# Hybrid attention layer: x's first tile on ScalarE's queue, the first weights rounded on VectorE, loads of x and weights in turn, and an order planned with the trace's figures

## The chip, the cores and the metric

The kernel runs on one core of one Trainium2 chip. The metric is device microseconds of one execution. The kernel before took 437.04 us, the median of three runs (436.71 to 437.82).

## The reference

One decoder layer on x of 512 tokens by 1024 channels, in float32. x is RMS-normalised and multiplied by one large input projection `w_in`; the result is cut into the inputs of two attention mixers and their gates.

```python
h = rms_norm(x, norm_w[l])
proj = h @ w_in[l]
o_a = moba_mixer(rms_norm(heads(q_a), ...), rms_norm(heads(k_a), ...), heads(v_a), bias_a)
k_cmp = rms_norm(compress(heads(kc), ...), k_norm_cmp[l]); v_cmp = compress(heads(vc), ...)
o_b = nsa_mixer(rms_norm(heads(q_b), ...), k_cmp, v_cmp, ..., heads(vwn), gate_b, bias_b)
y_a = o_a * jax.nn.silu(z_a); y_b = o_b * jax.nn.silu(z_b)
g_m = jax.nn.sigmoid(gate_m)
merged = g_m[..., :D] * (y_a @ w_branch_a[l]) + g_m[..., D:] * (y_b @ w_branch_b[l])
x = x + merged @ w_out[l]
```

Mixer A has 8 heads of 64 channels over all earlier tokens, with a relative-position bias; mixer B has 8 heads in two groups and three branches (compressed, selected and window), each with its own keys and values, summed with sigmoid gates. At 512 tokens the choice of blocks takes in every earlier block, so both mixers are causal attention with a bias, and B has a short compressed branch besides.

## The kernel before

**Precision.** Products that must be exact to float32 are made of three: every operand is split into a rounded part ("hi", written by a cast) and a remainder ("lo", written by a subtraction), and TensorE adds hi·hi, lo·hi and hi·lo into one PSUM tile (`mm3`, L420 to L434). So each weight tile of 128 x 512 costs one cast (L396, on ScalarE), one subtraction on VectorE (L406) and its matmuls. x is split in the same way, eight tiles of 128 channels by 512 tokens (`x_split`, L506 to L513), into `hh` and `hl`, with `norm_w` multiplied in. The division by the rms is applied later, to the results.

**Stages.** A few small matmuls on a tile of zeros stand first (L502, `NWARM` of them). Then comes the first projection, `qk0` (`gemm_first`, L683), which walks over the eight k tiles as they arrive: per tile four matmuls hi·hi, four with x's lo, four with the weights' lo. The others follow in the list `ORDER` (L632): token projections (`qk1`, `v`, `qb`, `kb`, `vb`) through `gemm_tok`, channel ones (`kc`, `vc`, the gates `za0` to `zb3`) through `gemm_chan`. Two entries of the list are not projections: `bias` makes the rows of the relative-position table (`bias_rows`, L863, one matmul, then a store to DRAM from which each head's table T is loaded), and `rows` spreads 1/rms over all partitions (`x_rows`, L577, two matmuls). Then come, per 128 output channels, a merge gate and a branch product (`gmgate`, `branch`, the loop at L1422 for A and at L1425 for B), and the output projection in seven products (L1568 on).

Attention runs between these. A unit is one head of A or one head and branch of B (24 in all). Per block of 128 queries: scores in PSUM (L1094, or L1092 for two branches at once), bias added and the minimum taken on VectorE (L1114), exp on ScalarE (L1125), hi and lo of the probabilities (L1132 and L1136), a DMA transpose, and the product with v (L1149). After a unit's last block `o_out` scales the output, and `y_try` multiplies in the gate and splits it for the branch product (L1187 to L1194). The first branch product of B waits for all of B's outputs.

**What sets the order.** The instruction order on every engine is fixed when the program is built, by a small simulation in the kernel itself. Each chain of operations (`Chain`) carries a cost in nanoseconds per engine ("A" ScalarE, "D" or "d" VectorE, "P" or "p" GpSimd), and a heap issues what is ready first. DMAs have a model of their own (`dma`, L231): issue time on SP, 1000 ns, then the transfer one after the other, 1700 ns to arrive. TensorE's order is the loop at L1637: several generators (`Run`) such as projections F, scores A, values V wait for conditions; of those whose condition holds since at least their margin (`MARGIN` 300 ns, `LATE_A` for scores, `LATE_V` for values, `LATE_S` for the scales of v), the one with the least virtual time goes next. If none has waited that long, the one that became ready first goes. Engines then run their lists in order and wait on semaphores for data, so a wrong cost changes no result but can put an instruction where its data is not there yet.

**Loads.** All DMAs are issued by SP. Weight tiles come through `Stream` (L331): `bufs` limits how far loads run ahead. At the start the loads stand in the order x0, w0, x1, x2, w1, x3, x4, w2, x5, x6, w3, x7, w4 (L499 and L1619 to L1625). x0 brings `norm_w` in 8 more columns.

Of the kernel before, what the change touches and what calls it, by code (L numbers as in the profile page):

```python
# [47 lines left out]
NRAW = 6  # L48
NWARM = 38
LAT = 60  # L50
# [8 lines left out]
MARGIN = 300  # L59
LATE_A = 1000  # L60
LATE_V = 1500
LATE_S = 1000
# [41 lines left out]
def hybrid_kernel(ctx: ExitStack, tc: tile.TileContext, x, x0, xT, wtok, wchan, gains, w1,  # L104
# [125 lines left out]

    def dma(dst, src, n, t=None):  # L231

        nc.sync.dma_start(out=dst, in_=src)
        t = issue(now[0] if t is None else t, 420)
        free["Q"] = max(free["Q"], t + 1000) + max(450, n * P / 360)
        return free["Q"] + 1700
# [94 lines left out]
    class Stream:  # L331


        def __init__(w, tiles, bufs, hi, lo):
            w.tiles, w.bufs, w.mk_hi, w.mk_lo = tiles, bufs, hi, lo
            w.raw, w.out, w.chain, w.i, w.loaded, w.ahead, w.next = {}, {}, {}, 0, 0, 0, 0

# [41 lines left out]
        def split(w, upto):  # L379
            for i in range(w.next, min(upto, len(w.tiles))):  # L380
# [13 lines left out]
                def f(e, hi=hi, raw=raw):  # L394
                    if e is nc.scalar:
                        e.copy(hi, raw)  # L396
                    else:
                        e.tensor_scalar(hi, raw, 1.0, 1.0, op0=ALU.mult, op1=ALU.mult)
                c.do({"A": ca(n)}, f).mark((w, 0, i))
                if squares:  # L400
# [50 lines left out]
    nrx = cp.tile([P, NT], F32, name="nrx")  # L451
    R = cp.tile([P, S], F32, name="R")
    nc.scalar.activation(R[:, :8], mhalf, AF.Exp)
    kcs = cp.tile([P, 2, 2, C32], F16, name="kcs")
# [20 lines left out]
    def rsqrt_mean(c, dst, ss, n, w, parts=P):  # L475
        v = (lambda z: z() if callable(z) else z)
        c.do({"D": 70}, lambda e: e.tensor_scalar(v(ss), v(ss), 1.0 / n / QS ** 2, EPS / QS ** 2, op0=ALU.mult, op1=ALU.add))  # L477
        c.do({"p": 430 + 150 * w}, lambda e: e.tensor_tensor(v(dst), v(ss), mhalf[:parts, :w], op=ALU.pow))  # L478

# [10 lines left out]

    first = alloc("dst", "x0", (P, 2048))
    xts = [first[:, :S]] + [att("x", F32) for _ in range(1, KT)]
    xat = {}

    def load_x(k):
        xat[k] = dma(xts[k], xT[(k - 1) * P:k * P, :], 2048)

    now[0] = 700.0
    xat[0] = dma(first[:, :S + KT], x0, 2080)  # L499
    Chain(xat[0]).do({"p": 140}, lambda e: e.tensor_copy(w8, first[:, S:S + KT]))  # L500
# [130 lines left out]

    ORDER = "qk0 bias v rows kc vc qk1 za0 kb qb za1 vb za2 za3 zb0 zb1 zb2 zb3".split()  # L632
    ORDER_T = [n for n in ORDER if n not in ("bias", "rows")]
    tiles = []
    for n_ in ORDER_T:
        tiles += tok_tiles(n_) if n_ in tlay else chan_tiles(n_)
# [198 lines left out]
    def proj_v(name, tags="gggg"):  # L835
        toks[name], per, i = [None] * NT, 1 + (name == "vb"), int(name == "vb")
        n = S // per

        def emit(t, ps):
            if t % per == 0:  # L840
                two = att(name, F32).bitcast(F16)
                toks[name][t:t + per] = [two[:, 2 * n * k:2 * n * (k + 1)] for k in range(per)]
            z = toks[name][t].rearrange("p (h s d) -> p h s d", s=2, d=DH)
            src, r = ps[:, :n].rearrange("p (h d) -> p h d", d=DH), rv[:, i, t:t + 1]
            ch = Chain(now[0] + 230, held=("vs", name) not in done)
            if ch.held:
                vwait[name].append(ch)
            else:
                ch.t = max(ch.t, done["vs", name])
            ch.do({"A": 145 + 0.834 * n}, lambda e: e.activation(z[:, :, 0, :], src, AF.Copy, scale=r))  # L850
            ch.do({"D": 65 + 1.045 * n}, lambda e: e.scalar_tensor_tensor(  # L851
                z[:, :, 1, :], src, r, z[:, :, 0, :], op0=ALU.mult, op1=ALU.subtract), ps).mark(f"{name}.{t}")
        yield from gemm_tok(name, emit, tags)
# [28 lines left out]
    def load_bias(h):  # L882
# [4 lines left out]
        t = dma(T, bass.AP(tensor=row.tensor, offset=row.offset + P - 1,  # L887
                           ap=[[16 * TW - P // NG, NG], [-1, P // NG], [1, S]]), 2048)
        return T, t
# [146 lines left out]
    class Unit:  # L1036
# [70 lines left out]
        def bias(u, c, b, sps, frees, T, last=False):  # L1107
            z, L, st = {}, P * (b + 1), u.stats()

            def f(e):  # L1110
# [5 lines left out]
                if last:  # L1116
                    release(T, c.t)
            c.do({"D": cd(L)}, f, frees, "sb")
            return z
# [44 lines left out]
    def o_out(O, m, h):  # L1164
# [14 lines left out]
        def f(e):  # L1179
            e.scalar_tensor_tensor(y[row:row + 64, :], O[0:64, :], r[0:64], z["t"], op0=ALU.mult, op1=ALU.add)  # L1180
            release(O, ch.t)
        ch.do({"D": 602}, f, lambda: z["t"])
        if row:
# [222 lines left out]
    def gemms():  # L1406
        for n in ORDER:
            if n == "rows":
                yield from x_rows()
            elif n == "bias":  # L1410
                yield from bias_rows()
            elif n == "v":
                yield from proj_v("v", "ttto")
# [4 lines left out]
            elif n[0] == "z":  # L1418
                yield from zgate(n[1], int(n[2]))
            else:  # L1420
                yield from proj_norm(n, n == ORDER_T[0], "ttto" if n == ORDER_T[1] else "gggg")
        for j in range(8):  # L1422
# [195 lines left out]

    W.bufs += 1  # L1619
    for k in range(1, KT):  # L1620
        if k % 2:
            W.load()
        load_x(k)
    W.load()
    W.bufs -= 1  # L1625
    for k in range(KT):
# [6 lines left out]
    Z = Run(starts(), 100.0)  # L1633
    U = Run(itertools.chain(v_scale("v", "s"), v_scale("vb", "t")), 100.0, LATE_S)
    Y = Run(itertools.chain(*sides), SHARE_B)
    runs = [Z, X, U, B, V, A, Y, F, C]
    while any(r.live for r in runs):  # L1637
# [90 lines left out]
```

## Time and profile before

| what | value |
|---|---|
| median of the runs | 437.04 us |
| lowest, highest | 436.71, 437.82 us |
| the profiled execution | 437.77 us |
| its span, first to last instruction | 435.6 us |
| TensorE (PE) busy | 421.2 us, 97% |
| VectorE (DVE) busy | 367.5 us, 84% |
| ScalarE (ACT) busy | 309.6 us, 71% |
| GpSimd (POOL) busy | 33.4 us, 8% |
| DMA | 75.30 MB, 173 GB/s on average |
| granted TensorE clock | 0.999 |

The span is shorter than the execution's time by 2.17 us, which lie before the first and after the last instruction. Times in rows count from the span's start. In a timeline row stand start and length in microseconds, engine, source line, operation, the tile written and those read, shapes and the number of instructions merged; in brackets how long the engine was idle before and what ended that. PEld is TensorE's load of weights, which overlaps its matmuls; SPq and the like are the sequencers, where DMAs are issued. "Rounding" or "cast" in the text is the writing of a hi part.

### The profile page before, as it was taken

The numbers are of one execution on the slowest core, as the hardware profiler recorded it, in microseconds if no ns is written. First come the engines' busy times: TensorE is split into PE (matmuls) and PEld (weight loads), VectorE is DVE, ScalarE is ACT, GpSimd is POOL, SyncE is SP. The second block draws the span as 40 slices with busy tenths as digits, with TensorE's granted clock in tenths as the row PEclk, the third lists the DMA queues.
The fourth block names the chain that finished last, engine by engine and source line by source line (L and its number), as shares of the span: only waits on it lengthen the run. The fifth ranks groups of instructions, "written<-read, shape, count | busy, mean of one in ns | idle before, by whom it ended". The sixth has DMA issues, their size and how long they took to land.

```text
span 435.6 us, 7107 instructions
## 1 busy us (share of the span) xinstructions
PE 421.2 (97%) x2134; PEld 326.0 (75%) x2134; DVE 367.5 (84%) x952; ACT 309.6 (71%) x802; POOL 33.4 (8%) x37
## 2 busy tenths in 40 slices
PE   9999999999988999999999999989999999999996
PEld 7878776777956687877776666757778888888886
DVE  5969689999898989699999798879955877599993
ACT  7996668897896998378899888979842534354720
POOL 0026000113213221000000000000000000000000
PEclk9999999999999999999999999999999999999999
DMA  8852978679989989417769867786668399251143
GB/s 290 269 203 65 216 200 165 110 178 232 236 239 185 161 179 256 121 23 159 164 149 156 182 165 133 192 136 153 155 175 285 122 353 322 77 172 47 50 136 104
DMA packets 116693, 75.30 MB, mean 173 GB/s; under 512 B 89072, under 2 KB 92016, under 8 KB 116656
## 3 DMA queue, kind: packets, MB, share of 16 engines
q1 hardware_dynamic: 116656, 74.86, 68.2%
q8 instruction: 17, 0.28, 0.2%
q14 instruction: 20, 0.16, 0.1%
HBM read 51.11 MB, written 2.75 MB: 124 GB/s over the span
## 4 chain that ended last, share of the span: by engine, by line
PE 60%; DVE 21%; DMA 6%; ACT 6%; issue 4%; POOL 1%; SPq 1%; DVEq 0%; POOLq 0%
PE pgc L431 21%; PE pgt L431 12%; PE po L431 9%; PE pbr L431 8%; DMA dst<-sb 5%; PE pgf L694 5%; DVE sb L1114 4%; DVE wl L406 4%; DVE sb L1136 3%; PE O L1149 3%; PE sps L1094 3%; ACT wh L396 1%; ACT junk L404 1%; DVE vl L406 1%; DMA x<-in_xT 1%
## 5 line engine op out<-in xcount | busy, mean ns | idle before, releaser
L431 PE MATMUL pgc<-hh,wh 128*128 128x512 f32 x208 | 87.3, 419 | 0.0
L431 PE MATMUL pgc<-hl,wh 128*128 128x512 f32 x208 | 82.1, 395 | 0.0
L431 PE MATMUL pgc<-hh,wl 128*128 128x512 f32 x208 | 82.1, 395 | 0.0
L406 DVE TENSOR_TENSOR wl<-wr,wh 128x512 fp32r<-128x512 f32 (+1 forms) x112 | 72.7, 666 | 10.0 <-ACT wh L396 9.7
L396 ACT CAST wh<-wr 128x512 fp32r<-128x512 f32 (+1 forms) x112 | 64.9, 597 | 6.9 <-DMA wr<-in_wbr 4.4
L1125 ACT ACTIVATE sb<-sb,sst 128x512 f32<-128x512 f32 (+3 forms) x96 | 53.4, 556 | 20.5 <-DVE sst L1114 20.0
L1114 DVE CUSTOM_DVE_ANT_0 sb<-sps,T,gst 128x512 f32<-128x512 f32 (+3 forms) x96 | 51.6, 540 | 9.3 <-DMA dst<-sb 8.4
L431 PE MATMUL pgt<-wh,hh 128*128 128x512 f32 (+2 forms) x160 | 58.3, 365 | 0.5 <-DVE vb L851 0.3
L431 PE MATMUL pgt<-wl,hh 128*128 128x512 f32 (+2 forms) x160 | 56.3, 352 | 0.9 <-DVE wl L406 0.9
L431 PE MATMUL pgt<-wh,hl 128*128 128x512 f32 (+2 forms) x160 | 55.8, 349 | 0.0
L1132 ACT ACTIVATE sb<-sb,sst 128x512 f16<-128x512 f32 (+3 forms) x96 | 51.1, 553 | 6.3 <-DVE sst L1128 5.8
L1136 DVE SCALAR_TENSOR_TENSOR sb<-sb,sst 128x512 f16<-128x512 f32 (+3 forms) x96 | 51.4, 544 | 3.7 <-ACT sb L1132 3.3
L431 PEld LDWEIGHTS pgc<-hl,wh 128*128 128x128 f32 x208 | 39.0, 188 | 9.5
L431 PEld LDWEIGHTS pgc<-hh,wh 128*128 128x128 f32 x208 | 39.1, 188 | 8.9
L431 PEld LDWEIGHTS pgc<-hh,wl 128*128 128x128 f32 x208 | 39.1, 188 | 7.5
L1094 PE MATMUL sps<-qkt,qkt 128*128 128x384 f16 (+3 forms) x160 | 36.4, 318 | 3.4 <-DVE sst L1114 3.4
L478 POOL TENSOR_TENSOR nr<-nss,mhalf 128x8 f32<-128x8 f32 (+1 forms) x16 | 26.7, 1675 | 105.7 <-DVE nss L477 94.6
L431 PEld LDWEIGHTS pgt<-wl,hh 128*128 128x128 f32 x160 | 30.0, 188 | 5.9 <-DVE wl L406 2.0
L431 PEld LDWEIGHTS pgt<-wh,hh 128*128 128x128 f32 x160 | 30.1, 188 | 4.9 <-PE pgt L431 0.4
L431 PEld LDWEIGHTS pgt<-wh,hl 128*128 128x128 f32 x160 | 30.1, 188 | 3.4
L1094 PEld LDWEIGHTS <-qkt 128*128 128x128 f16 x160 | 11.3, 98 | 21.2 <-issue 12.2
L431 PE MATMUL pbr<-yh,wh 128*128 128x512 f32 x64 | 26.2, 409 | 0.0
(226 smaller groups left out, 789.1 us busy)
## 6 DMA issues: line engine op xcount, KB each, us to landing
wr<-in_wchan SPq DMA_DIRECT2D x52, 256.0 KB, 3.5
wr<-in_wtok SPq DMA_DIRECT2D x36, 256.0 KB, 4.1
wq<-in_wout SPq DMA_DIRECT2D x36, 256.0 KB, 3.7
T<-rtab SPq DMA_DIRECT2D x16, 256.0 KB, 4.1
wr<-in_w SPq DMA_DIRECT2D x16, 256.0 KB, 3.5
wr<-in_wbr SPq DMA_DIRECT2D x16, 256.0 KB, 3.9
xr<-in_x SPq DMA_DIRECT2D x8, 256.0 KB, 5.7
x<-in_xT SPq DMA_DIRECT2D x7, 256.0 KB, 4.8
```

The lines of the kernel that those rows point to most:

```text
L396: e.copy(hi, raw)
L404: d.do({"A": 190 + 0.834 * m}, lambda e, z=hi[:, o:o + m], y=junk[:, :m], g=g, acc=acc: e.activation(y, z.bitcast(F32), AF.Square, scale=g ...
L406: c.do(either(n), lambda e, hi=hi, lo=lo, raw=raw: e.tensor_sub(lo, raw, hi.bitcast(F32))).mark((w, 1, i))
L431: nc.tensor.matmul(dst, sts[i][a], mvs[i][b], start=(start and i == a == b == 0), stop=(stop and i == n - 1 and b == 1), skip_group_check= ...
L478: c.do({"p": 430 + 150 * w}, lambda e: e.tensor_tensor(v(dst), v(ss), mhalf[:parts, :w], op=ALU.pow))
L694: nc.tensor.matmul(ps[t][:, :n], (hl if a else hh)[:, k, t * P:(t + 1) * P], ws[k][b], start=(k == a == b == 0), stop=(k == KT - 1 and b = ...
L1094: nc.tensor.matmul(sps[:, :n].rearrange("p (t n) -> p t n", n=P), qs, k4[:, x, j, :b + 1], start=not x, stop=bool(x))
L1114: e.tensor_tensor_reduce(z["sb"], sps[:, :L], T[:, S - L:], scale=nrunscale, scalar=3e38, op0=ALU.add, op1=ALU.min, accum_out=st[:, 0, b:b ...
L1125: c.do({"A": 279 + 0.834 * L}, lambda e: e.activation(z["sb"], z["sb"], AF.Exp, bias=st[:, 0, b:b + 1], scale=-1.0, accum_out=st[:, 1, b:b ...
L1132: e.activation(z["pp"][:, :L], z["sb"], AF.Copy, scale=s_)
L1136: c.do({"d": 59 + cd(L)}, lambda e: e.scalar_tensor_tensor(z["pp"][:, L:], z["sb"], s_, z["pp"][:, :L], op0=ALU.mult, op1=ALU.subtract))
L1149: nc.tensor.matmul(out, v, u.moving(kb, i), start=(u.first and kb == i == 0), stop=(u.last and kb == 3 and i == 1 and not u.before))
```

## The change

- x's first tile is loaded by ScalarE's DMA queue, ahead of ScalarE's first activation; its issue costs SP nothing in the plan.
- The cast of the first weight tile (and of no other) goes to VectorE, at a planned 205 + 0.54 n ns.
- Loads of weights and x stand in turn: w0, x1, w1, x2, and so on, with up to six weight tiles ahead instead of five.
- `bias_rows` and `x_rows` leave the list `ORDER` and become runs of their own: the first ahead of the scales of v in run U, the second in a new run O_.
- In `ORDER`, `vb` moves behind `za2`.
- Planned costs: GpSimd's power 430 to 700 ns plus 150 per column, VectorE's score step and two more steps 57 ns longer, a table load twice as long in the queue.
- `LATE_A` goes from 1000 to 1300, `LATE_V` from 1500 to 2000, `NWARM` from 38 to 33.

```diff
-NWARM = 38
+NWARM = 33
-LATE_A = 1000
-LATE_V = 1500
+LATE_A = 1300
+LATE_V = 2000
-    def dma(dst, src, n, t=None):
-        nc.sync.dma_start(out=dst, in_=src)
-        t = issue(now[0] if t is None else t, 420)
+    def dma(dst, src, n, t=None, engine=None):
+        (engine or nc.sync).dma_start(out=dst, in_=src)
+        t = issue(now[0] if t is None else t, 0 if engine else 420)
...
+            w.first = hi is None or w.bufs > 2
...
-                c.do({"A": ca(n)}, f).mark((w, 0, i))
+                c.do({"D": 205 + 0.54 * n} if w.first and not i else {"A": ca(n)}, f).mark((w, 0, i))
...
+    now[0] = 700.0
+    first = alloc("dst", "x0", (P, 2048))
+    xat = {0: dma(first[:, :S + KT], x0, 2080, None, nc.scalar)}
     nc.scalar.activation(R[:, :8], mhalf, AF.Exp)
...
-        c.do({"p": 430 + 150 * w}, ...)          # rsqrt_mean
+        c.do({"p": 700 + 150 * w}, ...)
...
-    first = alloc("dst", "x0", (P, 2048))
-    xat = {}
-    now[0] = 700.0
-    xat[0] = dma(first[:, :S + KT], x0, 2080)
...
-    ORDER = "qk0 bias v rows kc vc qk1 za0 kb qb za1 vb za2 za3 zb0 zb1 zb2 zb3".split()
+    ORDER = "qk0 v kc vc qk1 za0 kb qb za1 za2 vb za3 zb0 zb1 zb2 zb3".split()
...
-            ch.do({"D": 65 + 1.045 * n}, ...)    # proj_v, lo part
+            ch.do({"D": 122 + 1.045 * n}, ...)
-                           ap=[[16 * TW - P // NG, NG], [-1, P // NG], [1, S]]), 2048)
+                           ap=[[16 * TW - P // NG, NG], [-1, P // NG], [1, S]]), 4096)
-            c.do({"D": cd(L)}, f, frees, "sb")   # score step, L1114
+            c.do({"D": 57 + cd(L)}, f, frees, "sb")
-        ch.do({"D": 602}, f, lambda: z["t"])     # o_out
+        ch.do({"D": 659}, f, lambda: z["t"])
...
-    W.bufs += 1
+    W.bufs += 2
     for k in range(1, KT):
-        if k % 2:
-            W.load()
+        W.load()
         load_x(k)
-    W.load()
-    W.bufs -= 1
+    W.bufs -= 2
...
-    U = Run(itertools.chain(v_scale("v", "s"), v_scale("vb", "t")), 100.0, LATE_S)
+    U = Run(itertools.chain(bias_rows(), v_scale("v", "s"), v_scale("vb", "t")), 100.0, LATE_S)
+    O_ = Run(x_rows(), 100.0)
-    runs = [Z, X, U, B, V, A, Y, F, C]
+    runs = [Z, X, U, O_, B, V, A, Y, F, C]
```

More of the change, by code (lines that the diff above doesn't have):

```diff
@@ L477, in rsqrt_mean @@
         c.do({"D": 70}, lambda e: e.tensor_scalar(v(ss), v(ss), 1.0 / n / QS ** 2, EPS / QS ** 2, op0=ALU.mult, op1=ALU.add))
-        c.do({"p": 430 + 150 * w}, lambda e: e.tensor_tensor(v(dst), v(ss), mhalf[:parts, :w], op=ALU.pow))
+        c.do({"p": 700 + 150 * w}, lambda e: e.tensor_tensor(v(dst), v(ss), mhalf[:parts, :w], op=ALU.pow))
     def pair(a, b):
@@ L630, in chan_tiles @@
         return [(wchan[cnames.index(name), i], 512) for i in range(2)]
-    ORDER = "qk0 bias v rows kc vc qk1 za0 kb qb za1 vb za2 za3 zb0 zb1 zb2 zb3".split()
-    ORDER_T = [n for n in ORDER if n not in ("bias", "rows")]
+    ORDER = "qk0 v kc vc qk1 za0 kb qb za1 za2 vb za3 zb0 zb1 zb2 zb3".split()
     tiles = []
-    for n_ in ORDER_T:
+    for n_ in ORDER:
         tiles += tok_tiles(n_) if n_ in tlay else chan_tiles(n_)
@@ L850, in emit @@
             ch.do({"A": 145 + 0.834 * n}, lambda e: e.activation(z[:, :, 0, :], src, AF.Copy, scale=r))
-            ch.do({"D": 65 + 1.045 * n}, lambda e: e.scalar_tensor_tensor(
+            ch.do({"D": 122 + 1.045 * n}, lambda e: e.scalar_tensor_tensor(
                 z[:, :, 1, :], src, r, z[:, :, 0, :], op0=ALU.mult, op1=ALU.subtract), ps).mark(f"{name}.{t}")
@@ L1407, in gemms @@
         for n in ORDER:
[L1408 to L1412, printed above, removed]
+            if n == "v":
                 yield from proj_v("v", "ttto")
@@ L1420, in gemms @@
             else:
-                yield from proj_norm(n, n == ORDER_T[0], "ttto" if n == ORDER_T[1] else "gggg")
+                yield from proj_norm(n, n == ORDER[0], "ttto" if n == ORDER[1] else "gggg")
         for j in range(8):
```

## The prediction

> **What bounds the kernel now.** I read the page first, then busy time in stretches of ten microseconds, then the timeline of the first ten, then the table of waits, and last the chain that ended last around 320 us.
>
> ```profile
> span 435.6 us, 7107 instructions
> PE 421.2 (97%) x2134; PEld 326.0 (75%) x2134; DVE 367.5 (84%) x952; ACT 309.6 (71%) x802; POOL 33.4 (8%) x37
> ...
> 120.00:130.00 10.00, 8.05 (x42) 5.74 (x42) 9.97 (x32) 10.00 (x34) 1.32 (x1) 1.00 0.83 233
> 130.00:140.00 10.00, 8.75 (x40) 6.12 (x40) 8.10 (x35) 6.65 (x22) 3.53 (x2) 1.00 0.91 199
> 190.00:200.00 10.00, 10.00 (x46) 7.47 (x45) 10.00 (x32) 9.74 (x29) 0.00 (x0) 1.00 0.40 86
> 340.00:350.00 10.00, 10.00 (x45) 8.09 (x44) 8.71 (x16) 4.44 (x9) 0.00 (x0) 1.00 0.57 169
> ```
>
> In the stretches the columns after the length are the busy time of PE, PEld, DVE, ACT and POOL. PE is the bound: 14.4 us of its span are idle. From 330 us on it never waits. Where attention runs (about 55 to 320 us) VectorE and ScalarE are as full as PE, and there PE loses time, 1.95 us between 120 and 130 alone. So two places can pay: the start, and PE's waits in the attention part. Work that merely moves on a busy PE pays nothing.
>
> **The start.** The timeline of the first microseconds:
>
> ```profile
> 0.74 0.39 SPq L233 DMA_DIRECT2D x<-in_x  x1
> 0.89 4.23 PE L503 MATMUL pw<-warm 128*128 128x128 bf16 x38 [0.89 <-POOL ones L444]
> 1.19 0.42 SPq L233 DMA_DIRECT2D wr<-in_wtok  x1
> 3.65 0.72 ACT L510 ACTIVATE hh<-x 128x512 fp32r<-128x512 f32 x1 [1.41 <-DMA x<-in_x]
> 4.28 0.62 ACT L396 CAST wh<-wr 128x512 fp32r<-128x512 f32 x1
> 4.40 0.75 DVE L511 SCALAR_TENSOR_TENSOR hl<-x,hh 128x512 fp32r<-128x512 f32 x1 [3.23 <-ACT hh L510]
> 4.95 1.22 PE L694 MATMUL pgf<-wh,hh 128*128 128x512 f32 x4
> 5.65 1.41 ACT L510 ACTIVATE hh<-x,x 128x512 fp32r<-128x512 f32 x2 [0.22 <-DMA x<-in_xT]
> 6.01 1.08 PE L694 MATMUL pgf<-wh,hl 128*128 128x512 f32 x4
> 6.93 1.08 PE L694 MATMUL pgf<-wl,hh 128*128 128x512 f32 x4
> 7.48 0.60 ACT L396 CAST wh<-wr 128x512 fp32r<-128x512 f32 x1
> 8.13 1.20 PE L694 MATMUL pgf<-wh,hh 128*128 128x512 f32 x4
> 9.17 1.07 PE L694 MATMUL pgf<-wh,hl 128*128 128x512 f32 x4
> ```
>
> ScalarE scales x's first tile (to 4.37), then rounds the first weights (4.28 to 4.90), and PE starts at 4.95. The second k step starts at 8.13, because its weights were rounded only at 7.48. Four matmuls normally take 0.92 (6.01 to 6.93); here 1.20 and then 1.04 pass (6.93 to 8.13 to 9.17), so 0.28 + 0.12 = 0.40 us are lost.
>
> *First weights on VectorE.* The cast leaves ScalarE (0.62) and lies beside the scaling of x, in VectorE's 3.23 us of idle time. The trace has no SBUF-to-fp32r TENSOR_SCALAR of 512 columns; its bounds are these two, one smaller from SBUF, one of this size from PSUM.
>
> ```profile
> L1401 DVE TENSOR_SCALAR gn<-gn,gst 128x320 f32<-128x320 f32 x1 | 0.4, 382 | 0.0
> L874 DVE TENSOR_SCALAR rt<-pR,gst 128x512 f32<-128x512 f32 x1 | 0.7, 746 | 0.0
> ```
>
> At 0.38 to 0.75 either end is hidden so long as the weights land some 0.03 us or more ahead of x. I take 0.5, nearer the SBUF row. The new first start is then set by x: its landing, 0.03, the 0.72 of scaling and some 0.05.
>
> *x's first tile on ScalarE's queue.* SP is free one issue earlier, 1.19 - 0.74 = 0.45, for the weights. Issuing costs ScalarE one step like SP's 0.39, before its table load; the 1.41 us it waits for x hides that, and if that cover went, 0.39 would come on top. When x lands is not to be seen from one queue. Now the tiles land like this:
>
> ```profile
> L233 SPq DMA_DIRECT2D x<-in_x x1: 393/393/393, 0.7 to 0.7; - x1
> DMA to landing us min/median/max: 2.9/2.9/2.9
> ...
> L233 SPq DMA_DIRECT2D wr<-in_wtok x1: 421/421/421, 1.2 to 1.2; - x1
> DMA to landing us min/median/max: 3.1/3.1/3.1
> ```
>
> x at 0.74 + 2.9 = 3.64, the weights at 1.19 + 3.1 = 4.29. With two queues x may land as now or, sharing the engines with the weights, as late as both tiles do now, 4.29. So PE starts between 3.64 + 0.80 = 4.44 (0.51 earlier) and 5.09 (0.14 later). I take 0.2 earlier, near the middle. The Trainium skill (DMA: Bandwidth & Descriptors, section Queues, rings and completion order) says that each of the 16 engines takes turns between queues that have work, packet by packet; no row here shows two such queues. By that rule x would come with the weights, and the start would not move or be 0.14 later.
>
> What 0.2 are worth depends on PE's pace there. The 38 warm matmuls of 128 columns take 4.23, 0.11 each; the real ones need 0.23 for 512 columns, 0.058 per 128. So PE runs at half pace until about 5.1, though the clock column shows 1.00, and the first four matmuls still need 1.06 against 0.92. If pace follows time, work before 5.1 counts half; if it follows the count of matmuls, 33 instead of 38 moves it. I take half: 0.1 us, bounds -0.14 and 0.51. The Trainium skill (TensorE: Matmul & The Clock Gate, Part 1) has it by time, about 4 us of sustained work from a cold start; the 0.11 us agree with its cold figure for 128 columns. By it a start 0.51 earlier would be worth only 0.26, and the five warm matmuls taken away cost nothing.
>
> *Loads in turn.* The second weights move from fifth to fourth tile. x's second tile stays third and lands at about 5.6 (ScalarE took it at 5.65); the next follows by a tile's time. A tile is 0.262 MB:
>
> ```profile
> 6.00:7.00 1.00, 1.00 (x6) 0.82 (x5) 0.60 (x1) 1.00 (x3) 0.00 (x0) 1.00 1.03 391
> ```
>
> 0.262 MB at 391 GB/s is 0.67 us, so the weights land near 6.3. ScalarE has hh to 6.36 and the cast to about 7.0; PE needs it at 4.75 + 2.9 = 7.65. The wait goes: 0.40 us. What is late next: two weight tiles more lie ahead of the last x tile and the constants, some 1.3 us on SP's queue. PE spends 12 x 0.23 = 2.8 us on a k step against 2 x 0.67 for its loads, and needs x's last tile at 4.75 + 7 x 2.8 = 24.4; that covers it.
>
> Start together: 0.1 + 0.40 = 0.5 us, bounds 0.26 and 0.91.
>
> **Rows of bias and of 1/rms.** They leave the written order and become streams that PE takes when ready.
>
> ```profile
> 28.57 0.50 PE L869 MATMUL pR<-oh,rel 64*128 64x512 f32 x1
> 29.00 0.50 PE L431 MATMUL pgt<-wh,hh 128*128 128x512 f32 x1
> ```
>
> The same three matmuls run in either case. The first costs 0.43 to the next start rather than 0.23; that 0.2 may be lost twice or not at all. The table is needed only with the first scores, after v. I take 0, bounds -0.2 and 0.2.
>
> **Corrected costs and margins.** The plan (an order written before the run) had the score step on VectorE at 65 + 1.045 n, 600 ns for 512; now 657. PE waits for that step:
>
> ```profile
> L1114 DVE CUSTOM_DVE_ANT_0 sb<-sps,T,gst 128x512 f32<-128x512 f32 x24 | 17.7, 737 | 0.9 <-DMA T<-rtab 0.5 <-DMA dst<-sb 0.3
> ...
> PE sps L1094 <- DVE sst L1114: 3.4, 7, 0.9
> PE hps L936 <- DVE vl L406: 1.3, 2, 0.7
> PE O L1149 <- DMA dst<-sb: 1.1, 1, 1.1
> PE sps L1092 <- DVE sst L1114: 0.9, 1, 0.9
> PE pgt L431 <- DVE wl L406: 0.9, 1, 0.9
> ```
>
> Columns: total, times, longest. Eight score waits cost 3.4 + 0.9 = 4.3 us, 0.54 each: the order puts a score's matmuls at a time when VectorE, later than planned, has not freed the PSUM buffer. The margin for scores rises from 1.0 to 1.3 us and each VectorE step ahead in the plan is 0.06 longer, so a score comes some 0.36 later in the order, behind projection matmuls that have their data: 8 x 0.36 = 2.9 us of cover at most. But VectorE is full there (9.97, 10.00), and time won from a score can come back as a wait for wl or vl, whose rows stand beside it. I take 60%, 1.8 us. Bounds: 4.3 if all go, and -1.5 if every other matmul order gets worse by about what the wl, vl and transpose rows are now worth by half (3.3 / 2).
>
> **vb behind za2.** The same work in another order; za2 is 24 matmuls, 5.6 us.
>
> ```profile
> 181.77 0.48 DVE L851 SCALAR_TENSOR_TENSOR vb<-pgt,rv,vb 128x256 f16<-128x256 f32 x1 [0.16 <-ACT vb L850]
> 183.53 0.92 PE L1094 MATMUL sps<-qkt,qkt 128*128 128x512 f16 x4
> 322.49 0.69 ACT L1176 ACTIVATE ot<-O,vst 64x512 f32<-64x512 f32 x1 [4.55 <-PE O L1288]
> 325.36 0.69 DVE L1192 TENSOR_TENSOR yl<-ys,yh 128x512 fp32r<-128x512 f32 x1
> 327.31 5.60 PE pgc L431 x24
> 332.91 2.74 PE pbr L431 x12
> ```
>
> Mixer B's scores begin 1.3 us after vb, and their last product yl is ready at 326.05. Its first user, the first branch product of B, stands at 332.91: slack 6.9 us. Scores 5.6 later still fit, by 1.3. I take 0.
>
> **Sum.** Start 0.5 + margins 1.8 = 2.3 us less. The profiled execution took 437.77 us (span 435.6 and 2.17 around it); it would become 435.5. It lies 0.73 above the median of the runs, 437.04, so the median becomes **434.7 us**.
>
> **Rivals.** A measurement of this kernel can tell 0.3%, 1.3 us, from no change: below 435.7 is faster, above 438.3 slower.
>
> 1. *Waits only move.* For it: VectorE at 10.00 of 10 between 190 and 200. Against: at 130 to 140 it has 1.9 us to spare while PE waits 1.25. Only the start is won: 437.04 - 0.5 = 436.5, within 0.3%.
> 2. *Mixer B ends too late.* One mechanism: vb 5.6 us later, and scores held back by the larger margin, 0.3 each over the 56 steps of B (16 units of 4, 8 pairs sharing one); if only a quarter of that (4.2 us) lands on VectorE as idle time, B's end moves by 9.8, past the 6.9 of slack, and the first branch product waits 2.9 us with nothing else to run. It decides from 6.9 us on. For it: only that slack is left, and ScalarE already idles 4.55 us ahead of the last output, so B's end is bound by what PE hands over. Against: the plan's shares may bring B forward. 437.04 - 0.5 + 2.9 = 439.4.
> 3. *The new order is better all over.* The transpose, wl and vl waits (3.3) and all score waits (4.3) go by some 80%, 6.1: 437.04 - 0.5 - 6.1 = 430.4. For it: these waits come from the same underpriced steps. Against: nothing in the change touches wl's price.
> 4. *x lands late* (the two-queue case): the start gives 0.26 instead of 0.5. It moves any of these by 0.24 and has no time of its own.
>
> **Chances.** Forecast 434.7, spread 433.2 to 436.2: 42%. Rival 1 20%, rival 2 23%, rival 3 15%. Of the forecast's share a fifteenth or so falls within 0.3%, and of rival 1 a tenth counts as faster: faster 0.39 + 0.02 + 0.15 = 0.56; within 0.3% 0.03 + 0.17 and little of rival 2, 0.21; slower 0.23. The range runs from 431.3, leaving out half of rival 3 (7%), to 439.0, leaving out about half of rival 2 (12%).
>
> **What would show it.** Start: the first rounding of weights on VectorE, the first real matmul between 4.44 and 5.09, and no gap at the second k step. Margins: the two score rows together at about 2.5 us instead of 4.3, with no growth of the wl and vl rows. Rival 2: a wait of PE for yl just ahead of the first branch product of B. I would be wrong if the start moves by more than a microsecond, or if the attention part changes by more than 5 us, since then it is the order as a whole and not these waits.

## The result, and the profile after

The changed kernel took 435.58 us (median of 22 runs, 431.54 to 438.53) beside 436.98 us of the kernel before in the same rounds (22 runs, 435.68 to 442.56). The ratio is 0.9937 with a 95% interval of 0.9917 to 0.9958: faster by some 2.7 us. Ratios in this document leave out runs that were disturbed, here three of the 22, between 438.2 and 438.6, and one of before at 442.56, and further down three of `rows_back` (440.4 to 442.8) and one of `x0_on_sp_warm35` (437.35). The two medians above lie only 1.4 us apart, the means of the runs in the ratio 2.5. A second set of six runs of the same kernel (`again`, below) gave 0.9934 [0.9910, 0.9958]. The forecast was 434.7; the ratio times 437.04 is 434.3.

The profiled execution took 436.23 us, its span 434.0 (before: 437.77 and 435.6). First the head of its page:

```profile
span 434.0 us, 7113 instructions
...
PE 421.8 (97%) x2129; PEld 326.4 (75%) x2129; DVE 367.1 (85%) x952; ACT 309.2 (71%) x802; POOL 35.0 (8%) x37
```

PE is idle 12.2 us of the span instead of 14.4, and busy 0.6 us longer. But the two stages that the prediction costed went opposite ways. The timeline of the start (start, length, instruction, idle time before it and what ended it):

```profile
0.73 0.41 ACTq L233 DMA_DIRECT2D x<-in_x  x1
0.74 0.39 SPq L233 DMA_DIRECT2D wr<-in_wtok  x1
0.89 3.70 PE L502 MATMUL pw<-warm 128*128 128x128 bf16 x33 [0.89 <-POOL ones L445]
...
4.53 0.43 DVE L399 TENSOR_SCALAR wh<-wr 128x512 fp32r<-128x512 f32 x1 [3.37 <-DMA wr<-in_wtok]
...
4.71 0.72 ACT L509 ACTIVATE hh<-x 128x512 fp32r<-128x512 f32 x1 [2.04 <-DMA x<-in_x]
...
5.49 2.07 PE L692 MATMUL pgf<-wh,hh 128*128 128x512 f32 x4 [0.90 <-ACT hh L509]
...
7.36 1.91 PE L692 MATMUL pgf<-wh,hl 128*128 128x512 f32 x4
...
9.06 1.66 PE L692 MATMUL pgf<-wl,hh 128*128 128x512 f32 x4
...
10.56 1.10 PE L692 MATMUL pgf<-wh,hh 128*128 128x512 f32 x4
```

The first rounding of weights is on VectorE (0.43 us), beside the scaling of x, as planned. But x is there only for 4.71, 1.06 us later than before (3.65), and the weights, issued 0.45 us earlier than before, also come later (4.53 against 4.28). PE starts at 5.49 instead of 4.95, after 0.90 us of idle time, and its first matmuls then run at about half pace: the first four take 1.87 us to the next start (5.49 to 7.36), before 1.06 (4.95 to 6.01). So the second k step begins at 10.56, not at 8.13, though no gap stands ahead of it any more. By the last matmul of this projection (31.68, before 28.64; the bias matmul, which followed it before, now lies inside) the profiled execution is 3.0 us behind. The rest, up to the last PE instruction, is 4.5 us shorter; 0.4 of that is the bias matmul that moved ahead. The waits of PE there (total, times, longest):

```profile
PE sps L1092 <- DVE sst L1112: 2.9, 6, 1.4
PE O L1147 <- DMA dst<-sb: 2.3, 3, 0.8
PE pgf L692 <- ACT hh L509: 0.9, 1, 0.9
...
PE pk L970 <- DVE gt L956: 0.8, 1, 0.8
PE O L1147 <- ACT sb L1123: 0.5, 1, 0.5
PE hps L934 <- DVE vl L407: 0.3, 1, 0.3
```

The score waits are 2.9 us instead of 4.3; the waits for wl are gone and that for vl went from 1.3 to 0.3; the waits for the transposed probabilities rose from 1.1 to 2.3. In stretches of ten microseconds (busy time of PE, PEld, DVE, ACT, POOL; then the granted clock):

```profile
120.00:130.00 10.00, 8.57 (x49) 6.44 (x48) 9.97 (x33) 9.51 (x30) 4.06 (x2) 1.00 0.93 253
130.00:140.00 10.00, 9.03 (x40) 6.48 (x38) 8.24 (x30) 8.07 (x27) 0.00 (x0) 1.00 1.04 220
```

PE was busy 8.05 and 8.75 there before. The end of mixer B in the timeline:

```profile
327.86 0.69 ACT L1174 ACTIVATE ot<-O,vst 64x512 f32<-64x512 f32 x1 [2.89 <-PE O L1286]
...
330.74 0.69 DVE L1190 TENSOR_TENSOR yl<-ys,yh 128x512 fp32r<-128x512 f32 x1 [0.69 <-ACT yh L1189]
...
331.16 0.39 PE L432 MATMUL pbr<-yh,wh 128*128 128x512 f32 x1
...
331.62 0.39 PE L432 MATMUL pbr<-yl,wh 128*128 128x512 f32 x1
```

The last output of B stands 5.4 us later than before (322.49). yl is ready at 331.43, and its first user begins at 331.62 without a wait: 0.2 us are left of the slack. Not all of the 5.4 us is due to the order, since this execution was 3.0 us behind after its start; in `again`, below, with the same order and a faster start, that output stands at 326.76, 4.3 us later than before.

### The profile page after: what moved, and what is told of

Same layout as the page of the kernel before. It is cut to its first block, busy times and chain, and to the rows that moved or that the text cites. A ratio compares the mean times of both kernels' runs of the same rounds, so it can differ in the third digit from the quotient of the medians.

```text
span 434.0 us, 7113 instructions
## 1 busy us (share of the span) xinstructions
PE 421.8 (97%) x2129; PEld 326.4 (75%) x2129; DVE 367.1 (85%) x952; ACT 309.2 (71%) x802; POOL 35.0 (8%) x37
## 4 chain that ended last, share of the span: by engine, by line
PE 71%; DVE 13%; DMA 9%; ACT 4%; issue 3%; SPq 0%; DVEq 0%
PE pgc L432 28%; PE pbr L432 9%; PE po L432 9%; PE pgt L432 9%; PE pgf L692 6%; DMA dst<-sb 5%; PE O L1147 5%; PE sps L1092 3%; DVE sb L1112 2%; DVE sb L1134 2%; DMA wr<-in_w 2%; DVE wl L407 2%; ACT sb L1123 1%; DMA x<-in_x 1%; DVE nraw L772 1%
## 5 line engine op out<-in xcount | busy, mean ns | idle before, releaser
L482 POOL TENSOR_TENSOR nr<-nss,mhalf 128x8 f32<-128x8 f32 (+1 forms) x16 | 28.2, 1766 | 101.8 <-DVE nss L481 55.8
```

The lines of the kernel that those rows point to most:

```text
L482: c.do({"p": 700 + 150 * w}, lambda e: e.tensor_tensor(v(dst), v(ss), mhalf[:parts, :w], op=ALU.pow))
```

## The experiments

The theories: *the terms* (each part is worth what its waits say: start 0.5, margins 1.8, the others nothing), and *the order as a whole* (the plan written before the run is sensitive to every cost in it; no part has a price of its own). `before` in a ratio is the earlier kernel in the same rounds. All these kernels compute the whole reference.

### The start: which queue, how many warm matmuls

`x0_on_sp`: the changed kernel with x's first tile back on SP's queue, the order of the instructions on every engine unchanged.

```diff
-        (engine or nc.sync).dma_start(out=dst, in_=src)
+        nc.sync.dma_start(out=dst, in_=src)
```

> The changed kernel with one thing undone: x's first tile is issued by SP again, as its first DMA; the order on TensorE, VectorE, GpSimd and, but for that DMA, ScalarE is the changed kernel's, and so is the order of the other loads. Theory (the two queues share the engines): in the profile of the changed kernel x's first tile landed at 4.69 us and the first real matmul stood at 5.49, after 0.9 us of idle TensorE; here x lands near 3.64 again, the first real matmul stands near 4.5 to 4.6 and follows the warm ones without a gap, and the first ten matmuls no longer take 0.427 each but 0.23 from about 5.2 on. That is 0.9 + 1.9 = 2.8 us less than the profile of the changed kernel, a median near 433. Rival (x's late landing was a chance of that one execution): the landing moves by less than 0.3 us and the median stays within 0.7 us of the changed kernel's 435.6.

Measured: 434.4 us (431.84 to 437.94, 12 runs), 0.9942 [0.9912, 0.9972]. Timeline:

```profile
3.63 0.72 ACT L509 ACTIVATE hh<-x 128x512 fp32r<-128x512 f32 x1 [1.39 <-DMA x<-in_x]
...
4.26 0.43 DVE L399 TENSOR_SCALAR wh<-wr 128x512 fp32r<-128x512 f32 x1 [3.10 <-DMA wr<-in_wtok]
...
4.84 1.17 PE L692 MATMUL pgf<-wh,hh 128*128 128x512 f32 x4 [0.24 <-DVE wh L399]
...
7.68 1.08 PE L692 MATMUL pgf<-wh,hh 128*128 128x512 f32 x4
```

and the second row of PE's waits:

```profile
PE O L1147 <- DMA dst<-sb: 2.6, 3, 1.1
```

With one queue both tiles land earlier, PE starts 0.65 us earlier at full pace and is 2.9 us ahead at the second k step; the first projection ends at 28.51, 3.2 us earlier. But the span is only 1.5 us shorter (the transpose waits are 0.3 longer), and over all runs the ratios do not differ. Part of the reason is in `again`, below: the slow start of the first profile is not the usual one.

`warm44`: the changed kernel with 44 warm matmuls, same order again.

```diff
-NWARM = 33
+NWARM = 44
```

> The changed kernel with 44 warm matmuls instead of 33, everything else in the same order. At 0.107 us each they last until about 5.55, just past the 5.49 at which the first real matmul could start. Theory (the gap of 0.9 us between the last warm matmul and the first real one keeps the clock gate shut): the real matmuls run at 0.23 us from the first or second on, instead of 0.427 until 10 us; 1.9 us less than the profile of the changed kernel, a median of 433.5 to 434.5. Rival (the half pace at the start comes from something else, such as time since the first matmul of 512 columns): the first ten still take 0.427, and the median is the changed kernel's or 0.1 above it.

Measured: 434.77 us (432.3 to 437.39, 12 runs), 0.9954 [0.9931, 0.9976]. x still comes by ScalarE's queue, in this execution for 4.29; PE starts at 5.07 with no idle time in its row, at full pace, and the second k step begins at 7.93. Again no difference in time; the transpose waits are 3.9 us here.

`x0_on_sp_warm35`: both together, with 35 warm matmuls.

```diff
-NWARM = 33
+NWARM = 35
-        (engine or nc.sync).dma_start(out=dst, in_=src)
+        nc.sync.dma_start(out=dst, in_=src)
```

> The changed kernel's order with x's first tile on SP's queue and 35 warm matmuls, which last until 4.63 us, near the 4.84 at which the first real matmul stood with x on SP. Theory (x's queue is worth half a microsecond at the start, and what it is worth at the end the waits for transposes decide): the first real matmul at 4.8 to 4.9 without half pace, a median of 433.5 to 434.7, 0.5 to 2 below the changed kernel on the same chip. Rival (the time won at the start is all given back): the same median as the changed kernel within 0.4.

Measured: 433.05 us (430.27 to 437.35, 6 runs), 0.9891 [0.9864, 0.9918], beside 0.9934 [0.9910, 0.9958] for the changed kernel in the same rounds. It is the fastest kernel run here and clearly faster than the one before; that it beats the changed one is not settled, since the intervals overlap and `x0_on_sp`, two warm matmuls apart, was no better. Its transpose waits are 3.8 us.

`again`: the changed kernel itself, in those rounds, with no edit.

> The changed kernel itself once more, beside the others on the same chip, to see how far its start differs from one execution to the next: x lands between 4.2 and 5.1, the first real matmul stands between 5.0 and 5.9, and the first ten take either 0.23 or 0.427 each. Median 434.5 to 436.

Measured: 433.53 us (432.49 to 435.68, 6 runs), 0.9934 [0.9910, 0.9958]. Its timeline:

```profile
4.40 0.72 ACT L509 ACTIVATE hh<-x 128x512 fp32r<-128x512 f32 x1 [1.73 <-DMA x<-in_x]
...
5.17 1.19 PE L692 MATMUL pgf<-wh,hh 128*128 128x512 f32 x4 [0.58 <-ACT hh L509]
...
8.04 1.07 PE L692 MATMUL pgf<-wh,hh 128*128 128x512 f32 x4
```

x comes by ScalarE's queue for 4.40, PE starts at 5.17 after 0.58 us of idle time and runs at full pace at once. So the half pace in the first profile, worth 2.5 us at the second k step, does not come with every execution: of the ten profiles with x on ScalarE's queue only one other has it, that of `costs_back`. Of the 2.8 us by which `again` is ahead at the end of the first projection (28.88 against 31.68), 1.2 are left in the span (432.8 against 434.0); its transpose waits are 3.6 us. Here PE is idle 13.6 us of the span, only 0.8 less than before, and busy 419.2, 2.0 less, of which 0.5 are the five warm matmuls left out (3.70 instead of 4.23). And beside this usual start, x on SP's queue is worth only 0.36 us at the second k step (8.04 against 7.68), less than the runs can tell.

### The order without the start, and the start without the order

`order_only`: costs, margins, vb behind za2 and the rows of the change, with the start of before.

```diff
-NWARM = 33
+NWARM = 38
...
-                c.do({"D": 205 + 0.54 * n} if w.first and not i else {"A": ca(n)}, f).mark((w, 0, i))
+                c.do({"A": ca(n)}, f).mark((w, 0, i))
...
-    xat = {0: dma(first[:, :S + KT], x0, 2080, None, nc.scalar)}
...
+    xat[0] = dma(first[:, :S + KT], x0, 2080)
...
-    W.bufs += 2
+    W.bufs += 1
...
-        W.load()
+        if k % 2:
+            W.load()
...
+    W.load()
...
```

> The changed kernel with the start of the kernel before: 38 warm matmuls, x's first tile as SP's first DMA, the first weights rounded on ScalarE, loads in the old turn and with five weight tiles ahead; the streams for the rows, vb behind za2, the corrected costs and the margins stay. The plan is made anew from these, so the later order may differ from the changed kernel's in places. Theory (the gain came from the order of the attention part, the start lost about 2 us in the profile): 432.5 to 434, better than the changed kernel, with the first matmul at 4.95. Rival (the start paid and the order did nothing): 436.5 or more.

Measured: 435.47 us (434.15 to 436.03, 12 runs), 0.9959 [0.9939, 0.9979]. The start of before, with its wait at the second k step, and still faster than before; the interval overlaps that of the whole change. The time lies between what the two theories gave and bears out neither. Its timeline shows rival 2's wait, ahead of the tenth of B's twelve branch products:

```profile
330.90 0.50 PE L432 MATMUL pbr<-yh,wh 128*128 128x512 f32 x1 [0.88 <-ACT yh L1190]
```

`start_only`: before with the start of the change alone.

```diff
-NWARM = 38
+NWARM = 33
...
-                c.do({"A": ca(n)}, f).mark((w, 0, i))
+                c.do({"D": 205 + 0.54 * n} if w.first and not i else {"A": ca(n)}, f).mark((w, 0, i))
...
+    xat = {0: dma(first[:, :S + KT], x0, 2080, None, nc.scalar)}
...
-    xat[0] = dma(first[:, :S + KT], x0, 2080)
...
-    W.bufs += 1
+    W.bufs += 2
...
-        if k % 2:
-            W.load()
+        W.load()
...
```

> The kernel before with only the change's start: x's first tile on ScalarE's queue, first weights rounded on VectorE, loads in turn, 33 warm matmuls; costs, margins, list and streams as before. Theory (the start loses where x comes late): 437 to 439.5, with x landing near 4.7 and half pace up to 8 to 10 us. Rival (the start pays its 0.5 us as predicted): 436.0 to 436.7.

Measured: 446.09 us (445.32 to 448.99, 6 runs), 1.0220 [1.0185, 1.0254]. An edit of the first ten microseconds costs 9.6 us, far outside both expectations, and its first projection ends at 29.08, only 0.44 us later than before. The plan starts from other times, so all that follows is ordered anew. Its waits of PE:

```profile
PE sps L1093 <- DVE sst L1113: 5.3, 6, 2.0
PE hps L935 <- DVE vl L407: 4.0, 4, 1.4
```

and some of its stretches:

```profile
128.00:130.00 2.00, 0.06 (x1) 0.00 (x0) 0.85 (x8) 2.00 (x6) 1.01 (x1) 1.00 1.06 300
...
136.00:138.00 2.00, 1.65 (x4) 0.76 (x3) 2.00 (x10) 1.49 (x5) 0.00 (x0) 0.50 0.86 258
138.00:140.00 2.00, 1.96 (x5) 1.57 (x6) 1.97 (x9) 1.12 (x3) 1.37 (x1) 0.50 0.50 128
```

After 2 us in which PE did nearly nothing the granted clock falls to 0.50 and stays there from 131.3 to 141.5, 10.2 us. Of all that follows this is what the prediction had not reckoned with.

### One part taken back at a time

`margins_back`:

```diff
-LATE_A = 1300
-LATE_V = 2000
+LATE_A = 1000
+LATE_V = 1500
```

> The changed kernel with LATE_A back at 1000 and LATE_V at 1500; the start is the same instruction for instruction. Theory (the prediction's: the larger margins carry most of the gain): TensorE's two rows of waits for the score step come back to some 4 us from 2.9, and the median is 1.5 to 2.5 above the changed kernel's, 437 to 438. Rival (any new plan throws the attention part by a few us either way, so no single part carries the gain): the score rows need not grow, and the median may lie anywhere from 433 to 441. The plan itself, made with its own costs, ends 2.9 us later than the changed kernel's plan.

Measured: 438.84 us (436.4 to 441.42, 12 runs), 1.0045 [1.0021, 1.0070]: slower than before, and 1.1% above the whole change. But the waits that the margins were to cure are no longer than with them. Waits, then stretches:

```profile
PE sps L1092 <- DVE sst L1112: 2.1, 5, 0.7
PE hps L934 <- DVE vl L407: 1.6, 1, 1.6
PE O L1147 <- issue: 1.4, 1, 1.4
PE O L1147 <- DMA dst<-sb: 1.4, 1, 1.4
PE sps L1090 <- DVE sst L1112: 1.0, 1, 1.0
```

```profile
102.00:106.00 4.00, 0.98 (x7) 0.56 (x6) 3.64 (x8) 2.24 (x8) 0.33 (x1) 1.00 0.66 137
...
107.00:108.00 1.00, 1.00 (x7) 1.00 (x6) 0.41 (x1) 0.65 (x1) 0.00 (x0) 0.50 0.70 216
108.00:109.00 1.00, 1.00 (x6) 1.00 (x5) 0.90 (x2) 0.73 (x4) 0.00 (x0) 0.50 1.01 283
```

Score waits 3.1 us beside 2.9. What stands out is one place, 102 to 106, where the hps and O waits stand together: PE works 0.98 of 4 us, and then 3.4 us at half clock.

`costs_back`: the planned costs of before.

```diff
-        c.do({"p": 700 + 150 * w}, ...)
+        c.do({"p": 430 + 150 * w}, ...)
...
-            ch.do({"D": 122 + 1.045 * n}, ...)
+            ch.do({"D": 65 + 1.045 * n}, ...)
...
-                           ap=[[16 * TW - P // NG, NG], [-1, P // NG], [1, S]]), 4096)
+                           ap=[[16 * TW - P // NG, NG], [-1, P // NG], [1, S]]), 2048)
...
-            c.do({"D": 57 + cd(L)}, f, frees, "sb")
+            c.do({"D": cd(L)}, f, frees, "sb")
...
-        ch.do({"D": 659}, f, lambda: z["t"])
+        ch.do({"D": 602}, f, lambda: z["t"])
```

> The changed kernel with the planned costs of before (power on GpSimd 430 + 150 per column, score step, v's remainder and output scaling without the added 57 ns, table load 2048). Theory (corrected costs put scores later, where their data is): score waits of TensorE grow from 2.9 by 0.5 to 1 us, and the median is 0.5 to 1 us above the changed kernel's, 436 to 436.6. Rival (each new plan throws the attention part): anywhere from 433 to 441. The plan itself ends 1.2 us earlier than the changed kernel's, since its steps are shorter.

Measured: 438.19 us (436.7 to 440.21, 12 runs), 1.0032 [1.0012, 1.0053]. Waits:

```profile
PE O L1147 <- DMA dst<-sb: 3.5, 3, 2.6
PE sps L1092 <- DVE sst L1112: 1.5, 4, 0.7
PE pgt L432 <- DVE wl L407: 1.2, 2, 1.0
```

With the underpriced score step back, the score waits are the shorter ones, 1.5 us. What stands out is a transpose wait of 2.6 us, after which the clock is 0.50 from 108.6 to 112.0; this profile also has the slow start, with its second k step at 10.21.

`vb_back`: vb ahead of za2 again.

```diff
-    ORDER = "qk0 v kc vc qk1 za0 kb qb za1 za2 vb za3 zb0 zb1 zb2 zb3".split()
+    ORDER = "qk0 v kc vc qk1 za0 kb qb za1 vb za2 za3 zb0 zb1 zb2 zb3".split()
```

> The changed kernel with vb ahead of za2 again, as before the change. Theory (the place of vb is worth nothing by itself, as the prediction had it): 435 to 436.5, with TensorE's first product for mixer B some 5 us earlier than 214 and the last one earlier too. Rival (each new plan throws the attention part): anywhere from 433 to 441; the plan itself ends 3.4 us later than the changed kernel's.

Measured: 437.03 us (435.83 to 439.42, 12 runs), 1.0015 [0.9995, 1.0035]. So the step that I put at 0 is worth 0.8% in this surrounding, though not through the end of B: with vb ahead again, B's last output came no earlier, at 329.20 beside 326.76 in `again`. What stands out in its profile lies between 169 and 179: a transpose wait, then 6.8 us at half clock.

```profile
169.00:172.00 3.00, 1.12 (x6) 0.63 (x6) 1.87 (x4) 1.14 (x2) 0.00 (x0) 1.00 0.48 116
...
173.00:174.00 1.00, 1.00 (x7) 0.95 (x5) 0.38 (x3) 0.68 (x1) 0.17 (x1) 0.50 0.00 0
...
178.00:179.00 1.00, 1.00 (x6) 1.00 (x6) 0.22 (x1) 0.00 (x0) 0.00 (x0) 0.50 0.78 291
```

`rows_back`: the rows of bias and of 1/rms in the written order again.

```diff
-    ORDER = "qk0 v kc vc qk1 za0 kb qb za1 za2 vb za3 zb0 zb1 zb2 zb3".split()
+    ORDER = "qk0 bias v rows kc vc qk1 za0 kb qb za1 za2 vb za3 zb0 zb1 zb2 zb3".split()
...
-    U = Run(itertools.chain(bias_rows(), v_scale("v", "s"), v_scale("vb", "t")), 100.0, LATE_S)
-    O_ = Run(x_rows(), 100.0)
+    U = Run(itertools.chain(v_scale("v", "s"), v_scale("vb", "t")), 100.0, LATE_S)
...
```

> The changed kernel with the rows of bias and of 1/rms back in the written list, after qk0 and after v. Theory (moving three matmuls pays nothing by itself): 435.2 to 436, with the table's rows stored some 2 us later and the first scores unmoved. Rival (each new plan throws the attention part): anywhere from 433 to 441; the plan itself ends 2.2 us later than the changed kernel's.

Measured: 436.81 us (433.83 to 442.81, 12 runs), 0.9959 [0.9934, 0.9983], not told apart from the whole change. But the ratio rests on nine of the runs, and the median of all twelve is that of before (436.62); no worth of this term is shown, and that it is 0 is not settled.

### Fifty nanoseconds

If the margin cures the waits, a step of 50 ns in it must be worth next to nothing. `la1250` and `la1350`:

```diff
-LATE_A = 1300
+LATE_A = 1250
```

> The changed kernel with the margin for scores at 1250 instead of 1300 ns. The order on TensorE is the same up to row 838 of 2513, where one score step and a few small products change places; the plan's own end is 1.4 us later. Theory (the order as a whole): the median lies 1 us or more from the changed kernel's in either direction. Rival (each part has its own worth): within 0.5 us of it, 435 to 436.

Measured: 433.18 us (431.66 to 434.22, 6 runs), 0.9915 [0.9893, 0.9937]; not told apart from the change in the same rounds (0.9934 [0.9910, 0.9958]); PE's order is that of the changed kernel up to its 838th of 2513 rows.

```diff
-LATE_A = 1300
+LATE_A = 1350
```

> The changed kernel with the margin for scores at 1350 instead of 1300 ns; the start is the same. A score step moves by one slot from TensorE's row 310 on, and the plan spreads the difference from there; its own end is 4.3 us later. Theory (the order as a whole carries the gain, no term of it): the median moves by 2 us or more, to 437.5 or above, about as much as when a whole part of the change is undone. Rival (the parts undone were worth what they cost): 50 ns of a margin that went up by 300 are worth a sixth of that part, 0.5 us at most: 435 to 436.

Measured: 439.93 us (438.37 to 442.69, 6 runs), 1.0081 [1.0051, 1.0111]; its order leaves that of the changed kernel at row 310. Waits, then stretches, of `la1350`:

```profile
PE O L1147 <- issue: 2.5, 1, 2.5
PE O L1147 <- DMA dst<-sb: 1.7, 2, 0.9
...
PE pbr L432 <- ACT yh L1189: 0.9, 1, 0.9
...
PE sps L1092 <- DVE sst L1112: 0.4, 2, 0.2
```

```profile
106.00:107.00 1.00, 0.00 (x0) 0.00 (x0) 1.00 (x4) 0.31 (x2) 0.00 (x0) 0.93 0.80 261
107.00:108.00 1.00, 0.22 (x1) 0.14 (x2) 0.62 (x2) 0.02 (x1) 0.00 (x0) 0.50 0.23 32
...
112.00:113.00 1.00, 1.00 (x6) 1.00 (x5) 0.92 (x4) 1.00 (x5) 0.00 (x0) 0.50 1.26 187
```

The larger margin has all but ended the score waits (0.4 us), just as the mechanism would have it, and this is the slowest but one of all the kernels: 6.4 us (1.0081 - 0.9934 = 1.47% of 437) for 50 ns. It has one wait of 2.5 us at 107, then 6.8 us at half clock, and rival 2's wait for yh.

### What the granted clock adds

Each timed run also gives the mean granted clock over its span. By kernel, the ratio beside the mean clock over the runs in it; the third column is the ratio above 0.9937, times 437 us, and the fourth the clock below 0.9993, times 435 us, which is what the clock can account for at most (a stretch at half clock does half the work, and lowers the mean in the same measure):

| kernel | ratio | mean clock | above the change, us | by the clock, us at most |
|---|---|---|---|---|
| x0_on_sp_warm35 | 0.9891 | 0.9994 | -2.0 | 0 |
| la1250 | 0.9915 | 0.9998 | -1.0 | -0.2 |
| again | 0.9934 | 0.9990 | -0.1 | 0.1 |
| the change | 0.9937 | 0.9993 | | |
| x0_on_sp | 0.9942 | 0.9985 | 0.2 | 0.3 |
| warm44 | 0.9954 | 0.9991 | 0.7 | 0.1 |
| order_only | 0.9959 | 0.9970 | 1.0 | 1.0 |
| rows_back | 0.9959 | 0.9979 | 1.0 | 0.6 |
| before | 1 | 0.9992 to 0.9996 | 2.8 | 0 |
| vb_back | 1.0015 | 0.9960 | 3.4 | 1.4 |
| costs_back | 1.0032 | 0.9970 | 4.2 | 1.0 |
| margins_back | 1.0045 | 0.9943 | 4.7 | 2.2 |
| la1350 | 1.0081 | 0.9930 | 6.3 | 2.7 |
| start_only | 1.0220 | 0.9890 | 12.4 | 4.5 |

So of what the five slowest orders lose beside the change, a quarter to a half can be half clock; the rest is not in the clock. Even with one and the same order it tells: of the changed kernel's 19 runs in the ratio two at a clock of 0.996 average 437.1 us, the other 17 average 434.5. But the clock does not explain why the change beats before, whose clock is as high. Nor do the waits alone: PE's idle time fell by 2.2 us in the first profile, but in `again` by 0.8, and there its waits for scores, transposes, vl and vh together were 8.0 us, beside 7.6 for scores, transposes, vl and wl before. Where the other microseconds of `again` went is open.

## Why the prediction was right or wrong

The time fell in the range, with its sign and nearly its size (434.3 against 434.7). The sum that led there did not hold, so that the two agree so closely is luck.

*Start, -0.5.* Wrong. The parts on VectorE and ScalarE came as worked out (0.43 for the rounding, 0.41 for the issue, both hidden), and the gap at the second k step went away as "the wait goes: 0.40 us" says. The failing step is "x at 3.64 to 4.29" and the first matmul "between 4.44 and 5.09": in the ten profiles with x on ScalarE's queue it lands between 4.26 and 5.09 and PE starts between 5.07 and 5.88; in the four with both tiles on SP's queue x lands between 3.45 and 3.64 and PE starts between 4.78 and 4.95. I took the upper bound from both tiles' landing now, and more was possible; the weights too came later (4.34 to 4.91, on one queue 4.09 to 4.28). Rival 4 was the true case and even too mild. The Trainium skill (DMA: Bandwidth & Descriptors, section Queues, rings and completion order), which has the engines take turns between queues, had spoken against this step; x and the weights now land within 0.2 us of each other, which agrees with it, but why both together need longer no run here shows. In numbers at the second k step, 8.13 before: the rest of the change's start with x on SP's queue gives 7.68, 0.45 less, about the 0.40 that I had for the loads in turn; ScalarE's queue takes 0.36 of that back in `again` (8.04) and 2.88 in the first profile (10.56). In all eight profiles with x on ScalarE's queue and full pace the second k step stands between 7.93 and 8.76. So the start is worth about nothing, not 0.5, and in the two slow ones it is 2.1 and 2.4 worse than before. The times cannot tell these apart: `x0_on_sp`, `warm44` and the change do not differ, and in the one pair of profiles of the change 1.6 of the 2.8 us lost at the start are made up later, where PE waits less for the transposes (2.3 us after the slow start, 2.6 to 3.9 in the four profiles of this order with an early one).

*Rows, 0.* Not contradicted: `rows_back` is not told apart, though its spread leaves room for more.

*Margins, -1.8.* In the profile of the change the rows did what was asked: 4.3 to 2.9 us, not quite to 2.5, with no growth of wl and vl; what came back came as transpose waits (+1.2), which I had not named among the rows to watch. Yet as a price of the time the mechanism fell. Without the margins (`margins_back`) the score waits are as short, 3.1; with the old price of the score step they are shorter, 1.5; with 50 ns more margin they are nearly gone, 0.4, and the time is 1.47% worse. A score wait of before was not a property of the margin but of one order among many. The step that failed is "eight score waits, 0.36 later, 60% of them": it costs a change of the order by the waits of the old order, while the plan deals all of them anew.

*vb behind za2, 0.* No wait followed, as forecast, but the slack was used up to 0.2 us instead of 1.3. That B ended 5.4 later for 5.6 is luck: it is 4.3 in `again`, and 6.7 in `vb_back`, where vb stands ahead. The term itself did not hold: taking it back costs 0.8%, with a transpose wait and half clock at 169 to 179. I had looked only at what is late next and not at what the moved work had covered.

*Rivals.* Rival 1 fell, as more than the start moved. Rival 2's wait is real, 0.9 us instead of 2.9, in `order_only` and `la1350`, whose orders put its user ahead of yh's end; in the change it was missed by 0.2 to 0.45 us. Rival 3 is nearest to what the runs show, that the order as a whole differs, only with 2.7 us instead of 6.6. I had named "the order as a whole" as the sign that I was wrong, and set it at 5 us of change in the attention part; 4.5 us came. The other sign, a start that moves by more than a microsecond, did show: 2.4 us at the second k step of that profile. The sum of what the three parts that can be told apart cost when taken back, 4.7 + 3.4 + 4.2 = 12.3 us, beside the 2.8 of all together, says it without any threshold: these are not parts of a sum. That one of them carries the gain by itself is ruled out, since taking back any one of the three loses it all; which feature makes an order good stays open. The plan's own end, the planner's clock behind its last step, is a weak guide: later than the change's (418.8) by 2.9 us for `margins_back`, 3.4 for `vb_back` and 4.3 for `la1350`, which are slower, but also by 4.2 for `order_only` (423.0) and 1.4 for `la1250`, which are not told apart from it, and earlier by 1.2 for `costs_back` (417.6), which is slower.

## What to carry to other kernels

Where an order is written ahead by a planner, an edit of one of its costs is a new draw of the whole order: price it by the spread of neighbouring draws (here 1.7% between margins 1250 and 1350), and before crediting a part, take that part back and step it by a trifle. Put the first two tiles on one queue, the one needed first ahead, unless a trace shows that two queues land them sooner; here that moved the landings, not clearly the time. And look at the granted clock behind every cluster of PE waits.

## What the runs showed of the hardware

*Two queues at the start are slower for both.* x's 0.26 MB tile, issued at 0.73 to 0.74 in every profile, landed 0.6 to 1.6 us later beside a weight tile on another queue than ahead of it on the same one, and the weight tile no earlier than before although issued 0.45 us sooner. The pair that differs in x's queue alone: x at 3.60 and the weights at 4.24 in `x0_on_sp`, 4.37 and 4.57 in `again`.

*The clock falls to half in the middle of a kernel on one core.* Eight of the fourteen profiles have a stretch at 0.50 there, of 3.4 us (`margins_back`, `costs_back`, `order_only`, `warm44`, twice in `rows_back`), 6.8 (`la1350`, `vb_back`) or 10.2 (`start_only`). The Trainium skill (TensorE: Matmul & The Clock Gate, Part 1) has a free-running window of about 3.4 us and a half clock after one idle window; the lengths agree. So do the places: the traces keep the granted clock as a list of stretches, and every change in it lies a whole number of times 3.413 us behind the first entry (`margins_back`: 4.17 and 106.57, 30 times). But no single wait here was longer than 2.7 us, so a window need not be wholly idle. Cut at these places, the profiles have 1744 windows at full clock. In the 20 that half clock followed, 9 in the middle and 11 around the last matmul, PE was busy for at most 52% of the window; in the 1724 others for at least 56%. The two on either side of the limit, in `rows_back` and `warm44`:

```profile
114.07:117.48 3.41, 1.78 (x12) 1.58 (x13) 2.04 (x7) 1.35 (x4) 0.23 (x1) 1.00 1.07 264
...
171.11:174.52 3.41, 1.91 (x17) 1.77 (x15) 2.07 (x6) 2.29 (x6) 0.00 (x0) 1.00 1.24 164
```

The limit is read from these traces alone; no run was made to test it. Every one of the stretches in the middle ended with a window that PE filled. Where the windows lie differs from one execution to the next, so one order can fall on either side: around 108 us PE was busy 1.70 of 3.41 us in a window of `warm44`, which lost its clock, and 2.07 in one of `again`, which has the same order behind the start and kept it.

*Pace at the start varies from one execution to the next.* With the same order, PE's first ten real matmuls took 427 ns each in one profile of the change and 231 ns in another, with idle gaps of 0.90 and 0.58 us before them. The gap is not the whole cause: `margins_back`, with 0.9, and `start_only`, with 1.29, ran at 231 ns at once, `costs_back`, with 0.86, did not. The clock column shows 1.00 in all of these first stretches, but the list of stretches begins later, at 10.29 in the change, 9.58 in `costs_back` and 3.86 to 5.30 in the twelve others. There the matmuls' spacing falls from half pace to full pace, so the column's 1.00 ahead of it is no reading. In `margins_back` it begins at 4.17, ahead of the gap. In the change the window that ended at 6.88 had the gap in it and PE busy for 74%, in `costs_back` the one to 6.17 for 75%, and the full clock came one window later; in the twelve others the last window before it had 79% or more. That the gap's place in the window decides fits this, and was not tested.
